# Longer rows for half of Q and K in a cross-covariance attention kernel

## The chip, the core and the metric

The kernel runs on one core of one Trainium2 chip. The metric is the device time of one execution in microseconds (us). Times are medians over several runs; beside them stands one profiled execution, from which all durations of single instructions come.

## The reference

For each of 8 x 12 = 96 heads, Q, K and V are 512 x 64 matrices in float32. The columns of Q and K are divided by their norms over the 512 rows, the 64 x 64 product of the two goes through a softmax over its last axis, and V is multiplied with the result:

```python
Q_norm = Q / (np.linalg.norm(Q, axis=-2, keepdims=True) + 1e-10)
K_norm = K / (np.linalg.norm(K, axis=-2, keepdims=True) + 1e-10)
attn = np.einsum('bhnd,bhne->bhde', Q_norm, K_norm)
attn = np.exp(attn - np.max(attn, axis=-1, keepdims=True))
attn = attn / (np.sum(attn, axis=-1, keepdims=True) + 1e-10)
return np.einsum('bhnd,bhde->bhne', V, attn)
```

Each of Q, K, V and the output is 12.58 MB, so that 37.75 MB are read and 12.58 MB are written.

## The kernel before, in words

**Units.** Four heads are a unit u (U = 24), two units a pair s (S = 12), two pairs a window w (W = 6, 16 heads each). A head's 512 rows lie on 32 partitions, 16 rows of 64 numbers on each (T = 16), so that a partition's share of Q or K of one unit is a contiguous stretch of 4 KB. V lies on 16 partitions a head, in stretches of 8 KB. The output is stored in stretches of 2 KB.

**Stages.** `load_qk` (L170) and `load_v` (L182) bring the inputs in, mostly 1 MB at a time, into the tiles `qk32` (3 buffers, a pair each) and `v32` (3 buffers). `cast_qk` (L196) writes q and k of a unit side by side, in bf16, into `qkb` (2 buffers), on VectorE. `grams` (L210) multiplies, for each head and each t, the 32 x 128 block [q|k] with itself: 64 matmuls a unit. The 128 x 128 sum holds the squared norms of the columns of q and k on its diagonal and q.k off it. It lies in the PSUM tile `gram`, four banks, one buffer, one pair at a time. `squares` (L222) and `sums` (L236) take the diagonals out on VectorE, `cross` copies the off-diagonal block on ScalarE, `powers` makes inverse norms as exp(-0.5 ln x) on ScalarE, `scale_k` (L248) scales the block on GpSimd, `logits` transposes it on TensorE, `exps` (L265) takes exponentials on ScalarE, and `normalise` (L272) divides by their sums on VectorE.

**V and the output.** `cast_v` makes bf16 of V, on GpSimd for the most part; `vtrans` transposes it on TensorE into a single-buffered PSUM tile, `vcopy` copies that to SBUF, `outs` (L298) multiplies with the attention, `ocopy` copies PSUM to the store tile `so` (13 buffers), and `store` writes 0.5 MB. The copies of one kind all go through `copy` (L162), whose lines L164, L166 and L168 are the ScalarE, the VectorE and the GpSimd form. For the last window, the quarters q >= TAIL of the transposed V are cut in halves, which use four further PSUM banks that become free when the last `gram` has been read (`late_pool`).

**Order.** All DMAs are issued by SyncE (SP in the profile), in one queue. The class `Order` lays out the program before it is emitted: every piece has a price on one or more engines, pieces that it comes after, and a rank (`R`); a simulated clock picks what starts next, and `BIAS` makes one engine less attractive than another. The resulting order on each engine is fixed, and each engine waits in that order. From pair `BOTH` (= 4) on, copies of the output and casts of V may go to either of two engines.

Of the kernel before, what the change touches and what calls it, by code (L numbers as in the profile page):

```python
# [8 lines left out]
F32 = mybir.dt.float32  # L9
BF16 = mybir.dt.bfloat16  # L10
# [3 lines left out]
D = 64  # L14
T = 16
# [87 lines left out]
def kernel(  # L103
# [12 lines left out]
    W = S // 2  # L116
    TAIL = 2
    WIDE = U - 1
    ONE = 3
    BOTH = S - 8  # L120

# [5 lines left out]

    Vu = V.rearrange("b h (p t) d -> (b h p) (t d)", t=2 * T).rearrange("(w r p) x -> w r p x", r=2, p=128)

# [7 lines left out]

    NB = dict(qk=3, v=3, vb=2, qkb=2, vt=2, so=13, sm=2, ab=4)
    const = ctx.enter_context(tc.tile_pool(name="const", bufs=1))
    qp = ctx.enter_context(tc.tile_pool(name="qp", bufs=NB["qk"]))  # L140
    vp = ctx.enter_context(tc.tile_pool(name="vp", bufs=NB["v"]))
    vbp = ctx.enter_context(tc.tile_pool(name="vbp", bufs=NB["vb"]))
    qkp = ctx.enter_context(tc.tile_pool(name="qkp", bufs=NB["qkb"]))
    vtp = ctx.enter_context(tc.tile_pool(name="vtp", bufs=NB["vt"]))
    sop = ctx.enter_context(tc.tile_pool(name="sop", bufs=NB["so"]))
# [3 lines left out]
    ps_o = ctx.enter_context(tc.tile_pool(name="ps_o", bufs=2, space=bass.MemoryType.PSUM))  # L149
    grams_only = ExitStack()  # L150
    ps_g = grams_only.enter_context(tc.tile_pool(name="ps_g", bufs=1, space=bass.MemoryType.PSUM))
    late = {}

    def late_pool():
# [3 lines left out]
        return late["p"]  # L158

    qk32, v32, vb, qkb, gram, scr, kq, n2, r8, kqs, rq, lg, ex, ab, vps, vt, po, so = ({} for _ in range(18))  # L160

# [7 lines left out]

    def load_qk(s, x, r):  # L170

        w, e = divmod(s, 2)
        if s not in qk32:
            qk32[s] = qp.tile([128, 2, 2, T, D], F32, name="qk32")
        if 2 * s + (r or 0) >= WIDE:
            nc.sync.dma_start(out=qk32[s][:, x, r].rearrange("p (m j) d -> p m (j d)", m=2), in_=(Qw, Kw)[x][U - 1])
        elif r is None:
            nc.sync.dma_start(out=qk32[s][:, x].rearrange("p r t d -> p r (t d)"), in_=(Qu, Ku)[x][w, e])
        else:
            nc.sync.dma_start(out=qk32[s][:, x, r].rearrange("p t d -> p (t d)"), in_=(Qu, Ku)[x][w, e, :, r])  # L180

# [14 lines left out]
    def cast_qk(u, x):  # L196
# [3 lines left out]
        nc.vector.tensor_copy(qkb[u][:, :, x * D:(x + 1) * D], qk32[s][:, x, r])  # L200

    def cast_v(eng, w, r, c):

        if w not in vb:
            vb[w] = vbp.tile([128, 2 * T, 2, D], BF16, name="vb")
        copy(eng, vb[w][:, c * T:(c + 1) * T, r], v32[w, r][:, c].rearrange("p (t d) -> p t d", d=D))

    def grams(u):


        s, r = divmod(u, 2)
        if r == 0:
            gram[s] = ps_g.tile([128, HU, 2, 2, 2 * D], F32, name="gram")
        for t in range(T if u < WIDE else J):
            for h in range(HU):
                if u < WIDE:
                    x = qkb[u][32 * h:32 * (h + 1), t, :]
                else:
                    x = qkb[u][64 * (h % 2):64 * (h % 2 + 1), J * (h // 2) + t, :]
                nc.tensor.matmul(gram[s][:, h, r, 0], x, x, start=(t == 0), stop=(t == (T if u < WIDE else J) - 1))  # L220

    def squares(s, n):  # L222

        if n == 0:
            scr[s] = small.tile([128, 2 * HU, D], F32, name="scr")
        half = (LO, HI)[n]
        nc.vector.scalar_tensor_tensor(  # L227
            out=scr[s][half], in0=gram[s][half, :, :, 0, half].rearrange("p h r d -> p (h r) d"), scalar=1e-20,
            in1=eye2[half, None, :].to_broadcast([D, 2 * HU, D]), op0=ALU.add, op1=ALU.mult,
        )  # L230

    def cross(eng, s):

        kq[s] = small.tile([128, 2 * HU, D], F32, name="kq")
        copy(eng, kq[s][HI], gram[s][HI, :, :, 0, LO].rearrange("p h r d -> p (h r) d"))

    def sums(s):
        n2[s] = small.tile([128, 2 * HU], F32, name="n2")
        nc.vector.tensor_reduce(out=n2[s], in_=scr[s], axis=mybir.AxisListType.X, op=ALU.add)  # L239

    def powers(s):

        ln = small.tile([128, 2 * HU], F32, name="ln")
        r8[s] = small.tile([128, 2 * HU], F32, name="r8")
        nc.scalar.activation(ln, n2[s], AF.Ln)
        nc.scalar.activation(r8[s], ln, AF.Exp, scale=-0.5)  # L246

    def scale_k(eng, s):  # L248
        kqs[s] = small.tile([128, 2 * HU, D], F32, name="kqs")
        (nc.vector if eng == "DVE" else nc.gpsimd).tensor_tensor(  # L250
            out=kqs[s][HI], in0=kq[s][HI], in1=r8[s][HI, :, None].to_broadcast([D, 2 * HU, D]), op=ALU.mult,
        )

    def scales_q(s):

        rq[s] = small.tile([128, HU], F32, name="rq")
        nc.scalar.copy(rq[s][LO], r8[s][LO, 0::2])
        nc.scalar.copy(rq[s][HI], r8[s][LO, 1::2])
# [64 lines left out]
    nc.gpsimd.tensor_tensor(out=eye2, in0=ident[:, :D], in1=ident[:, D:], op=ALU.add)  # L323

    abs_ = []
    for i in range(NB["ab"]):
# [4 lines left out]
    def size(key):  # L331
        if key[0] == "gr" and key[1] >= WIDE:
            return 64
        return 8 if key[0] == "vt" and key[-1] is not None else {"gr": 128, "lg": 8, "vt": 16, "ou": 16}[key[0]]

    plan = Order(size)
    X = 1.29
    R = dict(cq=2.5, gr=2.471, sq=0.756, kq=1, rd=3.457, pw=3.5, sc=1, rq=1.9, lg=5, ex=1.1, nm=2.545, cv=1.165, vt=0.9, vc=1.1, ou=2, oc=0.9)
    BIAS = dict(sc=-0.6, kq=5, cv=1, vc=-0.3, oc=0.6)
    QK_PACE, V_FROM, V_PACE, ST_LAG = 0.631, 0.0377, 0.7486, 1.5133  # L340

# [3 lines left out]
    def piece(key, engines, after, behind, rank, fn, *args):  # L345
        if key[0] in ("cv", "vc", "oc", "kq", "sc"):
            plan.add(key, engines, after, behind, rank, lambda eng: fn(eng, *args))
# [6 lines left out]

    def parts(s):
        return (0, 1) if s < ONE or s == S - 1 else (None,)

    def loaded(x, s, r):
        return ("l" + "qk"[x], s, r if len(parts(s)) == 2 else None)

    last = None
    for s in range(S):
        free = [back("cq", 2 * s + r, 2 * NB["qk"], x) for r in range(2) for x in range(2)]
        for r in parts(s):
            at = QK_PACE * (2 * s + (r or 0)) / U
            for x in range(2):
                key = loaded(x, s, r)
                piece(key, {"DMA": X if r is not None else 2 * X}, free, [last], at, load_qk, s, x, r)
                last = key
    for u in range(U):  # L370
        s, r = divmod(u, 2)
        piece(("cq", u, 0), {"DVE": 0.72}, [loaded(0, s, r), back("gr", u, NB["qkb"])], [back("cq", u, 1, 1)], R["cq"] + 0.01 * u, cast_qk, u, 0)
        piece(("cq", u, 1), {"DVE": 0.72}, [loaded(1, s, r)], [("cq", u, 0)], R["cq"] + 0.01 * u, cast_qk, u, 1)
        piece(("gr", u), {"PE": 1.6}, [("cq", u, 0), ("cq", u, 1), back("kq", s, 1)], [back("gr", u, 1)], R["gr"] + 0.01 * u, grams, u)
    for s in range(S):
        SM = NB["sm"]

        piece(("sq", s, 0), {"DVE": 0.70}, [("gr", 2 * s), ("gr", 2 * s + 1), back("rd", s, SM)], [], R["sq"] + 0.01 * s, squares, s, 0)
        piece(("sq", s, 1), {"DVE": 0.70}, [("gr", 2 * s), ("gr", 2 * s + 1)], [("sq", s, 0)], R["sq"] + 0.01 * s, squares, s, 1)
        piece(("kq", s), {"ACT": 0.60, "DVE": (0.70, BIAS["kq"])}, [("sq", s, 0), ("sq", s, 1), back("sc", s, SM)], [], R["kq"] + 0.01 * s, cross, s)  # L380
        piece(("rd", s), {"DVE": 0.69}, [("sq", s, 0), ("sq", s, 1), back("pw", s, SM)], [], R["rd"] + 0.01 * s, sums, s)
        piece(("pw", s), {"ACT": 0.5}, [("rd", s), back("rq", s, SM), back("sc", s, SM)], [], R["pw"] + 0.01 * s, powers, s)
        piece(("sc", s), {"POOL": (1.04, BIAS["sc"]), "DVE": 1.2}, [("pw", s), ("kq", s), back("lg", s, SM)], [], R["sc"] + 0.01 * s, scale_k, s)
        piece(("rq", s), {"ACT": 0.45}, [("pw", s), back("ex", s, SM)], [], R["rq"] + 0.01 * s, scales_q, s)
        piece(("lg", s), {"PE": 0.6}, [("sc", s), back("ex", s, 1)], [], R["lg"] + 0.01 * s, logits, s)
        piece(("ex", s), {"ACT": 1.30}, [("lg", s), ("rq", s), back("nm", s, NB["sm"])], [], R["ex"] + 0.01 * s, exps, s)
        piece(("nm", s), {"DVE": 1.12}, [("ex", s)] + [back("ou", s, NB["ab"], x) for x in range(4)], [], R["nm"] + 0.01 * s, normalise, s)
# [83 lines left out]
```

## Time and profile before

| | us |
|---|---|
| median of 3 runs (130.26 to 130.95) | 130.85 |
| the profiled execution's own time | 130.86 |
| its span, first to last instruction | 129.1 |
| VectorE (DVE) busy | 91.0 (71%) |
| TensorE (PE) busy | 77.8 (60%) |
| ScalarE (ACT) busy | 72.5 (56%) |
| GpSimd (POOL) busy | 37.3 (29%) |
| time of the DMA packets, as a share of 16 engines' span | 98.0% |

A busy time is the sum of an engine's instructions; for DMA it is the mean over the core's 16 DMA engines. The own time of the profiled execution stands 1.8 us above its span and is equal to the median.

### The profile page before, as it was taken

How to read it: one execution, taken by the hardware profiler on the slowest of the kernel's cores; microseconds unless marked ns; L12 is line 12 of the kernel's file. 1: busy time of each engine (PE TensorE's matmuls, PEld its weight loads, DVE VectorE, ACT ScalarE, POOL GpSimd, SP SyncE). 2: the span in 40 equal slices, each digit the busy share in tenths (PEclk: the TensorE clock that was granted, in tenths of full speed). 3: DMA queues.
4: the chain of work that ended last, by engine and by line, in shares of the span. 5: the costliest groups of instructions: out<-in, count | busy, mean ns of one | idle time of the engine just before them, and what ended most of it. 6: DMA issues, size and time to landing. Idle time of an engine off the chain costs nothing.

```text
span 129.1 us, 4881 instructions
## 1 busy us (share of the span) xinstructions
PE 77.8 (60%) x2128; PEld 63.3 (49%) x2128; DVE 91.0 (71%) x140; ACT 72.5 (56%) x220; POOL 37.3 (29%) x39
## 2 busy tenths in 40 slices
PE   0154384994837648967682986697785858382000
PEld 0144372773636537856572865486664746271000
DVE  3444649849999389699986798997999799830000
ACT  3000441569777085497783798383947969973000
POOL 3005406300813914043058003223463270300000
PEclk9999999999975685599999599655799999955555
DMA  4999999999999999999999999999999999999982
GB/s 133 389 430 410 432 399 409 408 416 409 422 406 411 404 408 410 402 413 430 410 414 406 416 415 418 405 420 415 405 410 403 405 399 406 402 407 406 408 312 75
DMA packets 15605, 50.64 MB, mean 392 GB/s; under 512 B 1120, under 2 KB 1632, under 8 KB 14176
## 3 DMA queue, kind: packets, MB, share of 16 engines
q1 hardware_dynamic: 15584, 50.34, 98.0%
q8 instruction: 16, 0.26, 0.8%
q14 instruction: 5, 0.04, 0.1%
HBM read 37.75 MB, written 12.58 MB: 390 GB/s over the span
## 4 chain that ended last, share of the span: by engine, by line
DMA 50%; DVE 16%; PE 10%; ACT 8%; issue 3%; SPq 1%; POOL 1%; ACTq 0%; POOLq 0%; DVEq 0%
DMA qk<-in_K_dram 21%; DMA v<-in_V_dram 15%; DMA qk<-in_Q_dram 14%; DVE qkb L200 7%; PE gram L220 6%; ACT so L164 3%; DVE scr L227 3%; DVE vt L166 2%; PE po L306 2%; DVE ab L278 2%; PE vps L289 2%; ACT ex L269 2%; ACT vt L164 2%; DVE n L239 1%; SPq L180 1%
## 5 line engine op out<-in xcount | busy, mean ns | idle before, releaser
L220 PE MATMUL gram<-qkb 32*128 32x128 bf16 (+1 forms) x1504 | 36.6, 259 | 21.7 <-DVE qkb L200 15.4
L200 DVE CAST qkb<-qk 128x1024 bf16<-128x1024 f32 x48 | 37.4, 799 | 11.7 <-DMA qk<-in_Q_dram 5.2
L220 PEld LDWEIGHTS <-qkb 32*128 32x128 bf16 (+1 forms) x1504 | 30.5, 116 | 26.8 <-DVE qkb L200 18.1
L168 POOL TENSOR_SCALAR vb<-v 128x1024 bf16<-128x1024 f32 x19 | 21.9, 1162 | 46.7 <-DMA v<-in_V_dram 46.4
L164 ACT COPY so<-po 128x512 f32<-128x512 f32 x45 | 25.0, 592 | 7.6 <-PE po L306 7.5
L164 ACT COPY vt<-vps 128x1024 bf16<-128x1024 bf16 (+1 forms) x18 | 17.8, 987 | 16.9 <-PE vps L289 16.8
L306 PE MATMUL po<-ab,vt 128*64 128x128 bf16 x384 | 21.3, 260 | 6.7 <-issue 2.8
L250 POOL TENSOR_TENSOR kqs<-kq,r 64x512 f32<-64x512 f32 x12 | 14.2, 1179 | 26.1 <-ACT r L246 14.1
L306 PEld LDWEIGHTS <-vt 128*64 128x64 bf16 x384 | 15.5, 131 | 10.8 <-issue 5.8
L289 PE MATMUL vps<-identb,vb 128*128 128x128 bf16 x192 | 16.7, 236 | 6.6 <-POOL vb L168 3.9
L227 DVE SCALAR_TENSOR_TENSOR scr<-gram,eye 64x512 f32<-64x512 f32 x24 | 16.5, 688 | 5.6 <-PE gram L220 5.3
L289 PEld LDWEIGHTS <-vb 128*128 128x128 bf16 x192 | 12.6, 105 | 9.6 <-POOL vb L168 4.9
L269 ACT ACTIVATE ex<-lg,rq 128x64 f32<-128x64 f32 x48 | 14.5, 322 | 2.8 <-PE lg L263 2.8
L164 ACT COPY kq<-gram 64x512 f32<-64x512 f32 x12 | 7.0, 581 | 14.4 <-DVE scr L227 14.0
L278 DVE TENSOR_TENSOR ab<-ex,rinv 64x256 bf16<-64x256 f32 x24 | 13.5, 560 | 0.6
L269 ACT ACTIVATION_READ_ACCUMULATOR ex<-lg,rq 128x1 f32 x48 | 10.2, 213 | 0.0
L263 PE MATMUL lg<-eye,kqs 64*128 64x64 f32 x48 | 6.6, 266 | 4.1 <-POOL kqs L250 2.8
L239 DVE TENSOR_REDUCE n<-scr 128x8 f32<-128x512 f32 x12 | 8.1, 678 | 0.1
L166 DVE COPY vt<-vps 128x1024 bf16<-128x1024 bf16 (+1 forms) x8 | 7.9, 1019 | 0.1
L263 PEld LDWEIGHTS lg<-eye,kqs 64*128 64x128 f32 x48 | 4.7, 162 | 6.0 <-POOL kqs L250 3.6
L166 DVE CAST vb<-v 128x1024 bf16<-128x1024 f32 x5 | 5.1, 1012 | 0.9 <-DMA v<-in_V_dram 0.9
L275 DVE RECIPROCAL rinv<-esum 128x4 f32<-128x4 f32 x12 | 2.1, 171 | 2.5 <-ACT ex L269 2.5
(15 smaller groups left out, 15.8 us busy)
## 6 DMA issues: line engine op xcount, KB each, us to landing
out_dram<-so SPq DMA_DIRECT2D x23, 512.0 KB, 10.2
v<-in_V_dram SPq DMA_DIRECT2D x11, 1024.0 KB, 17.9
qk<-in_Q_dram SPq DMA_DIRECT2D x8, 1024.0 KB, 18.2
qk<-in_K_dram SPq DMA_DIRECT2D x8, 1024.0 KB, 18.8
qk<-in_Q_dram SPq DMA_DIRECT2D x8, 512.0 KB, 12.1
qk<-in_K_dram SPq DMA_DIRECT2D x8, 512.0 KB, 12.5
v<-in_V_dram SPq DMA_DIRECT2D x2, 512.0 KB, 10.7
out_dram<-so SPq DMA_DIRECT2D x2, 256.0 KB, 9.1
```

The costliest lines, as they stand in the source:

```text
L164: nc.scalar.copy(o, i)
L166: nc.vector.tensor_copy(o, i)
L168: nc.gpsimd.tensor_scalar(out=o, in0=i, scalar1=1.0, scalar2=0.0, op0=ALU.mult, op1=ALU.add)
L200: nc.vector.tensor_copy(qkb[u][:, :, x * D:(x + 1) * D], qk32[s][:, x, r])
L220: nc.tensor.matmul(gram[s][:, h, r, 0], x, x, start=(t == 0), stop=(t == (T if u < WIDE else J) - 1))
L227: nc.vector.scalar_tensor_tensor(out=scr[s][half], in0=gram[s][half, :, :, 0, half].rearrange("p h r d -> p (h r) d"), scalar=1e-20, in1=e ...
L250: (nc.vector if eng == "DVE" else nc.gpsimd).tensor_tensor(out=kqs[s][HI], in0=kq[s][HI], in1=r8[s][HI, :, None].to_broadcast([D, 2 * HU, ...
L263: nc.tensor.transpose(l[:, h, :], kqs[s][HI, 2 * h:2 * h + 2].rearrange("p r d -> p (r d)"), eye2[HI])
L269: nc.scalar.activation(e[:, h, :], lg[s][:, h, :], AF.Exp, scale=rq[s][:, h:h + 1], accum_out=z[:, h:h + 1])
L278: nc.vector.tensor_tensor(out=a[half, :, half], in0=e[half], in1=ri[half, :, None].to_broadcast([D, HU, D]), op=ALU.mult,)
L289: nc.tensor.transpose(ps[:, c, n, :], vb[w][:, J * c + j].rearrange("p r d -> p (r d)"), identb)
L306: nc.tensor.matmul(po[s, x][e * D:(e + 1) * D, j].rearrange("p r d -> p (r d)"), v, ab[s][:, h, :])
```

## The change

Windows 2, 3 and 4 (48 heads) are now "big". Their Q and K are loaded with a head on 16 partitions, 32 rows on each, so that a partition's stretch is 8 KB; a pair `m` is then eight heads, and its two units are the two halves of each partition's rows. The 32 partitions of a matmul now hold two heads. `mask_q` writes two copies of the bf16 q, in each of which the rows of one of the two heads are zero, and `big_grams` multiplies [q|k] with the 128 columns of the two copies. That gives the norms of q and the products k.q of both heads, but no norms of k. Those come from `square_k` (squares of the float32 k, ScalarE), `fold_k` (sums over a partition's 32 rows, GpSimd or VectorE) and `norms_k` (a matmul that adds a head's 16 partitions). The later steps of a big window run once for 16 heads, where they ran once for 8.

The tile `qkb` has 4 buffers instead of 2, `so` 9 instead of 13. TAIL is 4 instead of 2, so that nothing of the last window is cut in halves and no further PSUM banks are used. BOTH is 0 instead of 4. The ranks, biases and paces of the plan have other values. The `gram` tile keeps its four banks; for a big window it holds all four units.

```diff
-    TAIL = 2
+    TAIL = 4
-    BOTH = S - 8
+    BIG = (2, 3, 4)
+    BOTH = S - 12
...
+    Vu, Qb, Kb = (
+        x.rearrange("b h (p t) d -> (b h p) (t d)", t=2 * T).rearrange("(w r p) x -> w r p x", r=2, p=128)
+        for x in (V, Q, K))
...
-    NB = dict(qk=3, v=3, vb=2, qkb=2, vt=2, so=13, sm=2, ab=4)
+    NB = dict(qk=3, v=3, vb=2, qkb=4, vt=2, so=9, sm=2, ab=4)
+    mqp = ctx.enter_context(tc.tile_pool(name="mqp", bufs=NB["qkb"]))
+    ksp = ctx.enter_context(tc.tile_pool(name="ksp", bufs=1))
...
+        if big(m):
+            nc.sync.dma_start(out=qk32[m][:, x].rearrange("p c t d -> p (c t d)"), in_=(Qb, Kb)[x][w, e])
...
+    def mask_q(u):
+        mqb[u] = mqp.tile([128, T, 2, D], BF16, name="mqb")
+        for a in range(2):
+            nc.vector.tensor_scalar(
+                out=mqb[u][:, :, a], in0=qkb[u][:, :, :D], scalar1=half_of[:, a:a + 1], scalar2=None, op0=ALU.mult)
+    def square_k(u):
...
+        nc.scalar.activation(ksq[m][:, c], qk32[m][:, 1, c], AF.Square)
+    def fold_k(eng, m, part):
+        e = nc.vector if eng == "DVE" else nc.gpsimd
+        if part == 0:
+            e.tensor_tensor(out=ksq[m][:, 0], in0=ksq[m][:, 0], in1=ksq[m][:, 1], op=ALU.add)
+            return
+        ksum[m] = small.tile([128, D], F32, name="ksum")
+        n = T // 2
+        while n:
+            o = ksq[m][:, 0, :n] if n > 1 else ksum[m][:, None, :]
+            e.tensor_tensor(out=o, in0=ksq[m][:, 0, :n], in1=ksq[m][:, 0, n:2 * n], op=ALU.add)
+            n //= 2
+    def norms_k(m):
...
+        nc.tensor.matmul(o[:, :, r], ksum[m], head_of, start=True, stop=True)
+    def big_grams(u):
...
+        for t in range(T):
+            for n in range(HU):
+                rows = slice(32 * n, 32 * (n + 1))
+                o = g[:, n, :4 * D].rearrange("p (a r d) -> p a r d", a=2, r=2)[:, :, r]
+                nc.tensor.matmul(o, qkb[u][rows, t], mqb[u][rows, t], start=(c == 0 and t == 0), stop=(c == 1 and t == T - 1))
+    def big_squares(w):       # VectorE, 64 x 1024
+    def big_cross(eng, w):    # ScalarE or VectorE, 64 x 1024
+    def big_sums(w):          # VectorE, 64 x 1024
+    def logs_k(w):            # ScalarE, Ln of the norms of k, 64 x 16
+    def big_powers(w):        # ScalarE, Ln of those of q, Exp of both
+    def big_scale_k(eng, w):  # GpSimd or VectorE, 64 x 1024
+    def big_scales_q(w):      # ScalarE, two copies
...
+    half_of, head_of: two reductions of ident on VectorE; eye4, tiny: a copy and a memset on GpSimd
...
-    BIAS = dict(sc=-0.6, kq=5, cv=1, vc=-0.3, oc=0.6)
-    QK_PACE, V_FROM, V_PACE, ST_LAG = 0.631, 0.0377, 0.7486, 1.5133
+    BIAS = dict(ka=5, sc=0, kq=5, cv=5, vc=0.3, oc=0.6)
+    QK_PACE, V_FROM, V_PACE, ST_LAG = 0.5767, 0.076, 0.5601, 1.0571
...
+        if m >= NB["qk"] and big(m - NB["qk"]):
+            free += [("ks", 2 * (m - NB["qk"]) + i) for i in range(2)]
...
+            wait, release = release, [("kQ", w), ("sQ", w), ("lK", w)] if big(m) else [("kq", m)]
...
+        if big(m):
+            piece(("mq", u), {"DVE": 0.66}, [("cq", u, 0), back("gr", u, NB["qkb"])], [], R["mq"] + 0.01 * u, mask_q, u)
+            free = [("ka", before, 1)] if i == 0 and before is not None else []
+            piece(("ks", u), {"ACT": 1.15}, [loaded(1, m, i)] + free, [back("ks", u, 1)] if i else [], R["ks"] + 0.01 * u, square_k, u)
+            if i == 1:
+                for n in range(2):
+                    piece(("ka", m, n), {"POOL": 2.15, "DVE": (1.15, BIAS["ka"])}, ..., R["ka"] + 0.02 * m, fold_k, m, n)
+                piece(("kn", m), {"PE": 0.3}, [("ka", m, 1)], [("gr", 4 * w + 3)], R["kn"] + 0.02 * m, norms_k, m)
+        piece(("gr", u), {"PE": 1.6}, [("cq", u, 0), ("cq", u, 1), ("mq", u) if big(m) else None] + wait, [back("gr", u, 1)],
+              R["gr"] + 0.01 * u, big_grams if big(m) else grams, u)
```

The new functions from `big_squares` on are given by their names, engines and sizes; each is one or two instructions of the kind that its counterpart before has.

## The prediction

> **What bounds the kernel now.** I read the page's DMA lines first, because the engines' shares (71% at most) name no bound.
>
> ```profile
> DMA  4999999999999999999999999999999999999982
> ...
> DMA packets 15605, 50.64 MB, mean 392 GB/s; under 512 B 1120, under 2 KB 1632, under 8 KB 14176
> ...
> q1 hardware_dynamic: 15584, 50.34, 98.0%
> ```
>
> From the second slice to the last but one, all 16 DMA engines are busy, and their packets take 98.0% of 129.1 us. 15605 less 14176 leaves 1429 packets of 8 KB and more: the 11 V loads of 1 MB have 11 x 128 = 1408 stretches of 8 KB, and the 21 packets of the instruction queues make up the rest. So a packet is a partition's stretch, and the rate by size can be read from stretches in which one kind of load is served. These lines are from the table of stretches (columns: stretch, its length, busy PE, PEld, DVE, ACT, POOL, PE clock, DMA share, GB/s):
>
> ```profile
> 18.00:26.00 8.00, 5.93 (x148) 4.69 (x150) 6.35 (x10) 3.20 (x13) 3.14 (x3) 1.00 1.02 408
> 42.00:50.00 8.00, 4.75 (x136) 3.98 (x136) 5.59 (x11) 4.29 (x14) 3.68 (x4) 0.71 1.02 401
> 62.00:66.00 4.00, 2.83 (x102) 2.34 (x100) 3.90 (x6) 3.34 (x6) 0.18 (x1) 1.00 1.00 415
> 34.00:95.00 61.00, 44.21 (x1216) 35.73 (x1204) 52.72 (x78) 41.36 (x129) 22.11 (x19) 0.78 1.02 412
> 95.00:118.00 23.00, 15.26 (x356) 12.32 (x355) 17.25 (x30) 18.67 (x57) 6.20 (x6) 0.88 1.05 405
> ```
>
> The DMA queue serves in order, and a 1 MB load lands 18 us after its issue (page, part 6). By the issue times, 18 to 26 and 42 to 50 carry Q and K in 4 KB stretches (408 and 401 GB/s), and 62 to 66 two V loads in 8 KB stretches (415). The last two lines are for the engines: in the middle VectorE is busy for 52.7 of 61 us, so DMA is the bound, but not by much. The chain of waits agrees: 50% of it is DMA, and from 32.5 to 91 us it runs over three loads end to end.
>
> How late may the engines be? The last copy of output ends at 117.4 us, the last store is issued at 119.3, and it needs 9.1 us (median of the two quarter stores) because the queue is full. The shortest load, with an empty queue, landed in 3.3 us. So the work at the end has about 9.1 - 3.3 = 5.8 us to spare.
>
> [...] the trace shows more, 401 to 408 against 415, 1.7 to 3.5%. [...] a cast behind the scaling on GpSimd (1.33 us from 49.92) starts at 50.36 and lasts 1.44 us, where its median is 0.69. [...] the trace's copy of 1024 from PSUM takes 1.01.
>
> ```profile
> L200 DVE CAST qkb<-qk 128x1024 bf16<-128x1024 f32 x48 | 37.4, 799 | 11.7 <-DMA qk<-in_Q_dram 5.2
> ...
> L250 POOL TENSOR_TENSOR kqs<-kq,r 64x512 f32<-64x512 f32 x12 | 14.2, 1179 | 26.1 <-ACT r L246 14.1
> ...
> L227 DVE SCALAR_TENSOR_TENSOR scr<-gram,eye 64x512 f32<-64x512 f32 x24 | 16.5, 688 | 5.6 <-PE gram L220 5.3
> ...
> L278 DVE TENSOR_TENSOR ab<-ex,rinv 64x256 bf16<-64x256 f32 x24 | 13.5, 560 | 0.6
> ```
>
> **The change, part by part.**
>
> *DMA.* 48 heads of Q and K are 12.58 MB, in 1536 packets instead of 3072. At 404.5 GB/s (between 401 and 408) they take 31.1 us, at 415 30.3: 0.8 us less. The ends: [...] 1.06 us by 401. Number, size and order of kinds of the DMAs on SP's queue stay, so this is on the path from end to end.
>
> *VectorE.* Added: 24 tensor_scalar of 1024 bf16. No row shows one. [...] Gone: 12 `squares` x 0.688 = 8.3 [...] 6 `sums` x 0.678 = 4.1 for 3 x 1.21 = 3.6. Sum +3.3 us.
>
> *ScalarE.* Added: 12 squares of 1024 x 1.04 = 12.5 us. Gone on balance: 0.5 of `cross` (6 x 0.581 for 3 x 1.01), 1.3 of `powers` less 0.7 for `logs_k`, 1.2 of `scales_q`. Sum +10.2.
>
> *GpSimd.* From `scale_k`, 1.04 us for 512 at best, an add costs 2.03 ns an element: 2.1 us for the first (1024), 2.2 for the ladder (960, and three more starts), 4.3 a pair, 25.8 for six. Three wide scalings for six take 0.9 away. [...]
>
> *The lock.* Now casts lose 48 x (799 - 694) = 5.0 us and `normalise` 24 x (560 - 422) = 3.3, 0.115 us for each of 72, with GpSimd busy 22.1/61 = 36%. With the folds it is (22.1 + 24.9)/61 = 77%, so at least 2.1 times the wait, 0.245, for 24 casts, 24 masks and 12 halves of `normalise`: 14.7, where 36 x 0.115 = 4.1 stood, thus +10.6. The upper end: the folds last twice as long, so the residual wait may double: +25. I take +11[...].
>
> *Sum in the middle stage (34 to 95).* VectorE and ScalarE are busy for 52.7 + 41.4 = 94.1 of 122 us. Added 3.3 + 10.2 + 11 = 24.5: 118.6. BOTH = 0 lets copies of 15 us (8.0 vt, 5.1 vb, 2.1 so on VectorE) move between them. The densest 10 us slice now (30 to 40) holds 9.42 + 8.16 = 17.6 of 20, 88%. At 88% the stage takes 118.6/(2 x 0.88) = 67.4 us, 6.4 late. Loads run ahead by more than a 1 MB load's 18 us, and stores fill in, so DMA is not starved there. The next stage has 17.3 + 18.7 = 36 of 46 us; at 88% it takes 20.5 for 23 and gives 2.5 back. Late at the end: 3.9 us.
>
> *Waits and buffers.* TAIL = 4: the last two quarters go through one bank, 0.62 + 1.01 + hops = 1.75 us each, about 1 us more than the halves. 3.9 + 1 = 4.9, inside 5.8. The first gram after a big window waits for squares, cross and the logs of k; behind it on TensorE stand transposes, logits and outs; K's landing to logs is 2 squares, 4.3 of folds, 0.3 and 0.25, about 7 us, which four cast buffers and an idle TensorE (60%) cover. `qk32` is freed only after ScalarE's squares too, 2.1 us, covered by the loads ahead. `ksq` has one buffer: a square waits for the last pair's fold, and output copies and exponentials wait behind it on ScalarE; folds take 4.3 of the roughly 10 us of a pair, so at zero unless GpSimd is late. `so` with 9: a store is issued each 1.29 us and lands after 10.2, so 8 are in flight; one is left for the copy, which then runs at DMA's pace. The six small matmuls (0.3 each) and constants cost nothing: VectorE idles 2.15 us before its first cast[...]; GpSimd idles until 11.15.
>
> So the gain of 0.8 stays: 130.86 - 0.8 = 130.1, and as the profiled execution equals the median, 130.1 for the runs too.
>
> **The rivals.**
>
> *The lock decides (slower).* One mechanism: folds on GpSimd hold VectorE's casts and masks. If the lock costs 18 us instead of 11 (midway to the upper end), the stage is 7/(2 x 0.88) = 4.0 us later: 8.9 - 5.8 = 3.1 beyond the slack, 133.2. It turns at 12.6 us of lock, 1.6 above my value. For it: VectorE at 86% already and waits that end with GpSimd's instruction. Against it: some 21 us of VectorE's idle time now end with an event of DMA, PE or ACT (its waits, summed), and part of the lock's wait falls into such gaps.
>
> *The gain is eaten (same).* [...] the end is late by up to a microsecond: 130.3 to 131.4, at 130.8.
>
> *Rows do nothing (same): the change doesn't do what it says.* If 415 against 404 comes from what runs beside it, no gain: 130.9. 60 to 80 us, which mixes sizes, shows 415 to 417 too, which speaks for this a little.
>
> *Nine store buffers with one square buffer (slower).* ScalarE blocked in turn by stores and folds: some 2 us, 132.
>
> **How the numbers follow.** Half a percent, 0.65 us, is about what a measurement of this kernel can tell from no change. Forecast 0.44 (of which 0.04 falls within 0.5%); eaten or nothing 0.18; lock 0.32; buffers 0.06. Faster 0.40, same 0.22, slower 0.38. The forecast's own range is 129.7 to 130.4; over all, 129.5 (gain 1.06 and a little from the tail) to 133.2, the lock's value.
>
> **What would show it.** Right: 1536 packets fewer under 8 KB, 415 GB/s where big loads are served, DMA at 9 in all slices, mask mean below 0.5 us, last output copy before 122 us and the last store still 5 us or more from issue to landing. Wrong: VectorE above 105 us with casts above 1.0 us on average and GpSimd over 60 us; DMA slices under 9 between 80 and 125 us; the chain of waits on GpSimd's folds instead of loads; or a last store that lands 3 us after its issue, which says that the engines set the end.

## The result, and the profile after

The changed kernel takes 146.64 us (median of 4 runs) against 130.90 for the kernel before (4 runs beside it): ratio 1.121, interval 1.114 to 1.128. The forecast was 130.1, the top of the range 133.2. Some runs of the kernels below took over 1.5% longer than the fastest of the same kernel; ratios leave them out, and where they would change a reading, they are given apart.

From the page of the changed kernel: the DMA slices and rates, the packets, the DMA queue, and four of the costliest groups.

```profile
DMA  5999999999999999999999999998699845247796
GB/s 181 370 411 428 402 413 410 419 414 423 412 414 412 419 409 430 409 420 426 396 432 421 364 406 402 335 338 304 152 347 406 307 150 218 80 149 290 282 373 214
DMA packets 14069, 50.64 MB, mean 350 GB/s; under 512 B 1120, under 2 KB 1632, under 8 KB 11104
...
q1 hardware_dynamic: 14048, 50.34, 88.9%
...
L212 DVE CAST qkb<-qk 128x1024 bf16<-128x1024 f32 x48 | 43.3, 937 | 6.2 <-DMA qk<-in_Q_dram 4.8
...
L237 POOL TENSOR_TENSOR ksq<-ksq 128x512 f32<-128x512 f32 (+2 forms) x18 | 20.8, 1154 | 1.4
L231 POOL TENSOR_TENSOR ksq<-ksq 128x1024 f32<-128x1024 f32 x6 | 15.0, 2503 | 11.8 <-ACT lnk L280 6.4
...
L218 DVE TENSOR_SCALAR mqb<-qkb,half_of 128x1024 bf16<-128x1024 bf16 x24 | 17.4, 765 | 0.2
```

The rows did what the diff says: 15605 - 14069 = 1536 packets fewer. But from the 26th slice (some 90 us) the rate falls, and from the 28th (98 us) the DMA engines' share too. VectorE is busy for 119.6 us instead of 91.0, GpSimd for 78.8 instead of 37.3. The same by stretch (columns as before: length, busy PE, PEld, DVE, ACT, POOL, PE clock, DMA share, GB/s):

```profile
34.00:95.00 61.00, 35.70 (x989) 29.76 (x982) 56.52 (x67) 35.12 (x74) 42.69 (x33) 0.76 1.01 407
95.00:118.00 23.00, 14.09 (x335) 11.79 (x335) 21.81 (x26) 12.62 (x31) 19.81 (x16) 0.63 0.83 292
118.00:140.00 22.00, 15.16 (x368) 11.88 (x356) 18.31 (x30) 19.98 (x66) 7.14 (x5) 1.00 0.59 219
```

In the middle, DMA is still full because loads had been issued ahead, but the engines do less: TensorE 989 matmuls where 1216 were done, ScalarE 74 instructions where 129 were (big windows need fewer of them: 92 in e1 below). ScalarE is not short of time (35.1 of 61 us); VectorE nearly is (56.5), and GpSimd has doubled. The debt comes due mostly when only stores are left: the last store is issued at 140.0 us, where it was at 119.3.

The chain of waits, followed back from the end, has changed owner; these are its shares of the span before and after:

```profile
DMA 50%; DVE 16%; PE 10%; ACT 8%; issue 3%; SPq 1%; POOL 1%; ACTq 0%; POOLq 0%; DVEq 0%
```

```profile
DVE 51%; DMA 27%; PE 12%; issue 3%; ACT 1%; SPq 1%; DVEq 0%
```

Here is a piece of the timeline of the changed kernel, VectorE and GpSimd alone (columns: start, length, engine, line, operation; other engines' lines are left out):

```profile
98.61 2.26 DVE L212 CAST qkb<-qk 128x1024 bf16<-128x1024 f32 x2
98.84 5.28 POOL L175 TENSOR_SCALAR vb<-v 128x1024 bf16<-128x1024 f32 x4
...
101.38 1.84 DVE L218 TENSOR_SCALAR mqb<-qkb,half_of 128x1024 bf16<-128x1024 bf16 x2
...
103.14 1.52 DVE L212 CAST qkb<-qk 128x1024 bf16<-128x1024 f32 x1
104.09 2.77 POOL L231 TENSOR_TENSOR ksq<-ksq 128x1024 f32<-128x1024 f32 x1
104.70 3.24 DVE L286 TENSOR_TENSOR kqs<-scr,r 64x1024 f32<-64x1024 f32 x1
```

A cast of 0.69 us (median in the kernel before and in this one) lasts 1.52 while GpSimd casts V; the wide scaling, which the plan has moved to VectorE here, starts in a fold of 2.77 us and lasts 3.24, where it takes 1.58 without folds (e1 below). This lengthening is what the prediction and the expectations call the lock. That GpSimd holds something that VectorE needs was the author's assumption; the runs show how long the instructions take.

### The profile page after: what moved, and what is told of

It reads as the page before. It is cut to its first block, busy times and chain, and to the rows that moved or that the text cites. A ratio compares the mean times of both kernels' runs of the same rounds, so it can differ in the third digit from the quotient of the medians.

```text
span 144.8 us, 4941 instructions
## 1 busy us (share of the span) xinstructions
PE 81.2 (56%) x2140; PEld 67.2 (46%) x2140; DVE 119.6 (83%) x160; ACT 78.9 (55%) x210; POOL 78.8 (54%) x70
## 2 busy tenths in 40 slices
DMA packets 14069, 50.64 MB, mean 350 GB/s; under 512 B 1120, under 2 KB 1632, under 8 KB 11104
## 4 chain that ended last, share of the span: by engine, by line
DVE 51%; DMA 27%; PE 12%; issue 3%; ACT 1%; SPq 1%; DVEq 0%
DMA qk<-in_Q_dram 22%; DVE qkb L212 18%; DVE mqb L218 10%; DMA qk<-in_K_dram 5%; DVE kqs L286 4%; DVE ab L376 4%; DVE so L173 4%; PE gram L260 4%; DVE vt L173 3%; DVE scr L264 2%; PE vps L387 2%; PE po L404 2%; PE gram L317 2%; DVE n L273 2%; ACT so L171 1%
## 5 line engine op out<-in xcount | busy, mean ns | idle before, releaser
L175 POOL TENSOR_SCALAR vb<-v 128x1024 bf16<-128x1024 f32 x24 | 31.3, 1325 | 11.6 <-DMA v<-in_V_dram 11.4
L317 PE MATMUL gram<-qkb 32*128 32x128 bf16 (+1 forms) x736 | 18.5, 272 | 16.2 <-DVE qkb L212 16.2
L171 ACT COPY so<-po 128x512 f32<-128x512 f32 x35 | 19.5, 590 | 10.6 <-PE po L404 10.3
L317 PEld LDWEIGHTS <-qkb 32*128 32x128 bf16 (+1 forms) x736 | 16.0, 123 | 17.9 <-DVE qkb L212 17.3
L171 ACT COPY vt<-vps 128x1024 bf16<-128x1024 bf16 x18 | 18.2, 1014 | 9.0 <-PE vps L387 9.0
L237 POOL TENSOR_TENSOR ksq<-ksq 128x512 f32<-128x512 f32 (+2 forms) x18 | 20.8, 1154 | 1.4
L231 POOL TENSOR_TENSOR ksq<-ksq 128x1024 f32<-128x1024 f32 x6 | 15.0, 2503 | 11.8 <-ACT lnk L280 6.4
L367 ACT ACTIVATE ex<-lg,rq 128x64 f32<-128x64 f32 x48 | 14.5, 317 | 12.5 <-PE lg L361 12.3
L260 PE MATMUL gram<-mqb,qkb 32*128 32x128 bf16 x768 | 17.6, 259 | 4.8 <-DVE qkb L212 3.3
L348 POOL TENSOR_TENSOR kqs<-scr,r 64x512 f32<-64x512 f32 x5 | 5.4, 1084 | 25.0 <-ACT r L344 16.6
L260 PEld LDWEIGHTS <-qkb 32*128 32x128 bf16 x768 | 15.3, 116 | 6.3 <-DVE qkb L212 3.8
L218 DVE TENSOR_SCALAR mqb<-qkb,half_of 128x1024 bf16<-128x1024 bf16 x24 | 17.4, 765 | 0.2
L225 ACT ACTIVATE ksq<-qk 128x1024 f32<-128x1024 f32 x12 | 12.5, 1058 | 7.8 <-POOL ksum L237 7.8
## 6 DMA issues: line engine op xcount, KB each, us to landing
v<-in_V_dram SPq DMA_DIRECT2D x11, 1024.0 KB, 15.8
```

What stands on the lines that cost most here:

```text
L171: nc.scalar.copy(o, i)
L175: nc.gpsimd.tensor_scalar(out=o, in0=i, scalar1=1.0, scalar2=0.0, op0=ALU.mult, op1=ALU.add)
L218: nc.vector.tensor_scalar(out=mqb[u][:, :, a], in0=qkb[u][:, :, :D], scalar1=half_of[:, a:a + 1], scalar2=None, op0=ALU.mult)
L231: e.tensor_tensor(out=ksq[m][:, 0], in0=ksq[m][:, 0], in1=ksq[m][:, 1], op=ALU.add)
L237: e.tensor_tensor(out=o, in0=ksq[m][:, 0, :n], in1=ksq[m][:, 0, n:2 * n], op=ALU.add)
L260: nc.tensor.matmul(o, qkb[u][rows, t], mqb[u][rows, t], start=(c == 0 and t == 0), stop=(c == 1 and t == T - 1))
```

## The experiments

"Last store" is the issue of the last DMA of output in the profiled run; "VectorE" is its busy time there. The spread of the kernel before over these runs is 130.35 to 131.15 in its medians.

### The two halves of the change alone

**e4_rows_only.** The kernel before with

```diff
+        elif s // 2 in (2, 3, 4):
+            nc.sync.dma_start(out=qk32[s][:, x].rearrange("p r t d -> p (r t d)"), in_=(Qb, Kb)[x][w, e])
```

> The kernel before, loading Q and K of windows 2 to 4 in 8 KB stretches and computing on as if they lay as before, which mixes heads. It is the gain of the rows alone: 0.8 us less by the prediction (ratio 0.994), [...] none if the rate is set by something else.

Measured: ratio 0.9953 (0.9934 to 0.9972), 130.02 against 130.69 us: 0.61 us less, between 0.37 and 0.86. Its DMA slices are full throughout, as they were. The gain is real and was sized well.

**e3_before_buffers.** The kernel before with

```diff
-    TAIL = 2
+    TAIL = 4
-    BOTH = S - 8
+    BOTH = S - 12
-    NB = dict(..., so=13, ...)
+    NB = dict(..., so=9, ...)
-    grams_only = ExitStack()
+    grams_only = ctx.enter_context(ExitStack())
```

> The kernel before with 9 store buffers instead of 13, TAIL 4 and BOTH 0, and none of the longer rows. If buffers and tail are innocent, 130.5 to 132 us. If the nine buffers or the single bank carry the loss, 136 us or more.

Measured: ratio 1.0051 (1.0022 to 1.0079), 131.31 us. These three settings move the last store from 119.3 to 123.9 us and cost 0.7 us, not 15. Which of the three does it was not tried.

### The folds on GpSimd

**e1_short_folds.** All adds of `fold_k` but one of 64 elements are left out:

```diff
         if part == 0:
-            e.tensor_tensor(out=ksq[m][:, 0], in0=ksq[m][:, 0], in1=ksq[m][:, 1], op=ALU.add)
             return
...
-        n = T // 2
-        while n:
-            ...
+        e.tensor_tensor(out=ksum[m][:, None, :], in0=ksq[m][:, 0, :1], in1=ksq[m][:, 1, :1], op=ALU.add)
```

> The changed kernel with the sums of k's squares cut from five adds to one of 64 elements on GpSimd; the norms of k are left wrong by that, all else and the order on every engine stay. If the folds decide (by the lock or by their length), the 36 us of GpSimd work go, VectorE falls from 119.6 us busy to below 105, and the time to 129.5 to 133 us. If the nine store buffers, the single bank at the end or the new order decide, it stays at 143 to 147 us.

Measured: 130.83 us, ratio 0.9995 (0.9972 to 1.0018); VectorE 99.7 us, last store 123.1. The folds carry all of the loss. The middle stretch, with the columns of the table above:

```profile
34.00:95.00 61.00, 42.57 (x1203) 35.06 (x1199) 57.26 (x87) 43.74 (x92) 23.56 (x23) 0.81 1.02 414
```

VectorE is as busy there as with the folds, 57.3 us for 56.5, but it gets 87 instructions done instead of 67. The granted clock of TensorE isn't the cause: it was 0.764 to 0.787 in the runs of the changed kernel, but the profiled run of e1 had 0.768 and took 130.69 us.

Of VectorE's instructions none was taken away, and yet it is busy for 19.9 us less in the whole run. The two lines each are of VectorE's groups, the first pair from this kernel and the second from e2, where the folds run:

```profile
L212 DVE CAST qkb<-qk 128x1024 bf16<-128x1024 f32 x48 | 33.2, 726 | 8.5 <-DMA qk<-in_Q_dram 4.9 <-DMA qk<-in_K_dram 3.2
L218 DVE TENSOR_SCALAR mqb<-qkb,half_of 128x1024 bf16<-128x1024 bf16 x24 | 13.8, 616 | 0.2
```

```profile
L212 DVE CAST qkb<-qk 128x1024 bf16<-128x1024 f32 x48 | 43.3, 934 | 7.0 <-DMA qk<-in_Q_dram 3.9 <-DMA qk<-in_K_dram 2.7
L218 DVE TENSOR_SCALAR mqb<-qkb,half_of 128x1024 bf16<-128x1024 bf16 x24 | 19.4, 848 | 0.2
```

**e2_detached_folds.** The adds work on a constant tile, and the squares are written in bf16 and read by nobody, so that nobody waits for the folds:

```diff
+        ksum[m] = some_sum
-            e.tensor_tensor(out=ksq[m][:, 0], in0=ksq[m][:, 0], in1=ksq[m][:, 1], op=ALU.add)
+            e.tensor_tensor(out=spare, in0=spare, in1=spare, op=ALU.add)
...
-            e.tensor_tensor(out=o, in0=ksq[m][:, 0, :n], in1=ksq[m][:, 0, n:2 * n], op=ALU.add)
+            e.tensor_tensor(out=spare[:, :n], in0=spare[:, :n], in1=spare[:, n:2 * n], op=ALU.add)
```

> The changed kernel with the five adds on GpSimd kept in size and place, but working on a constant tile, so that nothing waits for them (the norms of k come from a constant; the squares are written in bf16 and read by nobody). Theory of the lock: GpSimd still holds VectorE's casts and masks, VectorE stays above 112 us busy, and the time stays at 140 us or more. Rival, that the chain squares, folds, norms, logs is too long: with nobody waiting for the folds the time falls to 129.5 to 134 us.

Measured: 143.68 us, ratio 1.100 (1.095 to 1.105); VectorE 118.3 us, last store 137.4. Without any wait for a fold, 12.9 of the 15.8 us between e1 and the changed kernel are there. Could it be GpSimd's own queue, the V casts and scalings behind the folds? These are all waits of TensorE for GpSimd in e2 (columns: engine, line, released by: us in total, times, longest):

```profile
PEld lg L360 <- POOL kqs L347: 2.8, 2, 2.4
...
PE lg L360 <- POOL kqs L347: 2.4, 2, 2.2
...
PEld L386 <- POOL vb L175: 1.3, 2, 0.9
...
PE vps L386 <- POOL vb L175: 0.9, 2, 0.6
```

In e1 the same four are 2.4, 2.0, 1.5 and 1.1, so TensorE doesn't wait longer for GpSimd. ScalarE waits for it in neither; the DMA queue waits 3.1 us for it in e2 and not at all in e1. What is left is that the same VectorE instructions take 18.6 us longer while GpSimd works: casts 10.1, masks 5.6, scalings 1.7, `normalise` 1.2. The other kinds are not longer: output copies, which read PSUM, take 687 ns in e1 and 686 in e2, `sums` 678 and 676, `squares` 688 in both. So it is these four kinds that get longer and not VectorE as a whole; by what means GpSimd does it, no run shows.

In the changed kernel the DMA queue waits 17.3 us for casts of V on GpSimd, and the last two V loads are issued from 101.8 us on, where it is 96.6 in e2: late folds hold up the casts behind them too.

**e6_no_masks.** The folds stay, and the masks go:

```diff
-            nc.vector.tensor_scalar(out=mqb[u][:, :, a], ...)
...
-                nc.tensor.matmul(o, qkb[u][rows, t], mqb[u][rows, t], ...)
+                nc.tensor.matmul(o, qkb[u][rows, t], qkb[u][rows, t, None, :D].to_broadcast([32, 2, D]), ...)
```

> The changed kernel without the 24 masks (the unmasked q is multiplied twice, which mixes two heads); folds stay on GpSimd. If it is VectorE that is late, the 17.4 us that the masks take on it go and the time falls by 10 us or more, to 130 to 136 us. If it is GpSimd that is late (its own queue of folds, V casts and scalings), the time stays at 142 us or more.

Measured: 139.18 us (the other run, 142.59); VectorE 99.3 us, last store 132.4. Both expectations fail: VectorE is no busier than in e1, and the kernel is still 8 us slower than the one before. The casts still take 0.91 us, and the waits show a second way:

```profile
ACT ksq L221 <- POOL ksum L233: 9.8, 4, 4.8
PEld gram L245 <- POOL ksum L233: 7.6, 3, 3.0
PE gram L245 <- POOL ksum L233: 7.2, 3, 2.9
```

Squares wait on ScalarE for the one `ksq` buffer, which the last fold still reads, and the norms of k wait on TensorE. So there is a second cause: the chain from squares over folds to the norms of k, whose folds GpSimd finishes late.

**e11_detached_no_masks.** e2 and e6 together.

> Folds detached as in e2 and masks left out as in e6, both together; it mixes heads and takes the norms of k from a constant. GpSimd keeps its 36 us of folds and the lock. If VectorE's lateness and the wait for the folds are two causes of which each alone holds the time above 140 us, taking both away gives 129.5 to 133 us. If GpSimd's own queue (V casts and scalings behind the folds) is a third, 137 us or more.

Measured: 135.98 us, ratio 1.039 (1.029 to 1.050); VectorE 106.5 us, last store 129.9. The four form a square: 146.6 (all), 143.7 (no chain), 139.2 (no masks), 136.0 (neither). The chain is worth 3.0 us with masks and 3.2 without, the masks 7.4 with the chain and 7.7 without; these differences are rough, for there is one run of e6 and the two of e11 lie 1.6 apart. The time lies between the two expected ranges, and some 5 us above e1 remain. They are again on VectorE: casts average 1.05 us, and TensorE's waits for GpSimd are those of e1 (1.9, 1.5, 1.5, 1.0 us), so the third cause that was offered isn't seen.

**e5_split_folds.** The same adds in pieces of at most 256 elements:

```diff
+            for q in range(4):
+                t = slice(4 * q, 4 * q + 4)
+                e.tensor_tensor(out=ksq[m][:, 0, t], in0=ksq[m][:, 0, t], in1=ksq[m][:, 1, t], op=ALU.add)
```

> The changed kernel with the folds on GpSimd cut into adds of at most 256 elements (about 0.5 us each instead of up to 2.1), same sums. If VectorE loses time because it waits for whole GpSimd instructions, shorter ones cost it less: casts fall from 0.94 us to below 0.85, VectorE from 119.6 to below 113 us, the time to 136 to 143 us. If the total of GpSimd's work is what counts, it stays at 144 us or more.

Measured: 148.11 us (the other run, 151.51); VectorE 113.3 us, last store 141.4. VectorE is busy for 6 us less, but casts stay at 0.91. GpSimd rises to 85.3 us, and squares wait 12.5 us for folds instead of 7.8. No remedy.

**e10_real_prices.** `{"POOL": (2.5, 4.3)[n], "DVE": (1.15, 9.0)}` instead of `{"POOL": 2.15, "DVE": (1.15, BIAS["ka"])}`.

> The changed kernel planned with GpSimd prices of 2.5 and 4.3 us for the two parts of a fold (2.15 and 2.15 in the change; the trace shows 2.5 and 3.9 plus gaps), and nothing else. If the loss comes from an order laid out for folds that take longer than planned, a plan with real prices wins back much of it: below 140 us. If the work and the lock themselves do not fit, 143 us or more.

Measured: 152.1 us, ratio 1.163 (1.153 to 1.173). A plan that knows how long folds last is worse. The bias against VectorE rose too, from 5 to 9, and the ranks had been made for other prices; which of these does it was not tried.

### The folds elsewhere

**e8_vector_folds.** `{"DVE": 1.15}` as the only engine.

> The changed kernel with the folds on VectorE alone. No lock from folds, [...] VectorE at 112 to 117 us busy. From 99.7 us with 130.8 and 119.6 us with 146.6, one us of VectorE is worth one us beyond about 104: 138 to 144 us. If only the lock mattered and not VectorE's own time, 131 to 134 us.

Measured: 155.85 us, ratio 1.191 (1.179 to 1.202); VectorE 122.0 us, beyond both. The order was laid out anew, so this mixes work and order.

**e7_tensor_folds.** Squares in bf16 with two buffers, no folds, and

```diff
-        nc.tensor.matmul(o[:, :, r], ksum[m], head_of, start=True, stop=True)
+        for c in range(2):
+            for t in range(T):
+                nc.tensor.matmul(o[:, :, r], ksq[m][:, c, t], head_ofb, start=(c == 0 and t == 0), stop=(c == 1 and t == T - 1))
...
-                for n in range(2):
-                    piece(("ka", m, n), ...)
-                piece(("kn", m), {"PE": 0.3}, [("ka", m, 1)], [("gr", 4 * w + 3)], ...)
+                piece(("kn", m), {"PE": 2.5}, [("ks", u - 1), ("ks", u)], [("gr", u)], ...)
```

> The changed kernel with the folds moved to TensorE: squares are written in bf16 and 32 matmuls a pair add over rows and partitions at once, so GpSimd has no folds. The result is complete. Lock theory: VectorE at 99 to 102 us busy and 130 to 132 us in all, like the kernel with the sums left out. Rival, that TensorE's queue becomes the bound with 192 more matmuls[...]: 134 us or more.

Measured: 140.82 us, ratio 1.079 (1.071 to 1.087); VectorE 102.0, GpSimd 40.3 us; the 192 matmuls keep TensorE busy for 8.2 us. Without folds on GpSimd the kernel is still slow; matmuls and order both changed here.

**e9_tensor_folds_same_order.** The same matmuls, with the `ka` pieces left in the plan but emitting nothing.

> The folds on TensorE as in e7, but planned at the changed kernel's prices for them, so that every engine keeps the changed kernel's order; the result is complete. If e7 was slow because the plan was laid out anew with ranks made for other prices, this one runs like the kernel with the sums left out, 130 to 132.5 us, with about 8 us more on TensorE. If the 192 matmuls themselves cost (TensorE late), 136 us or more.

Measured: 132.57 us (the other three, 135.78 to 137.08; no interval); in the profiled run, of 137.08 us, VectorE 105.0 us, last store 128.7. The kept order is worth 5 us or more against e7; e1's 130.83 isn't shown to be out of reach, but none of the four runs has it.

**e12_one_matmul.** e9 with one matmul a pair.

> e9 with one matmul a pair for the norms of k instead of 32, which leaves most of the sum out; squares, order and everything else stay. If the five us between e9 and the kernel with short folds are the 192 matmuls on TensorE (9.6 us busy), it falls to 130.5 to 132 us. If VectorE sets the time (105 us busy in e9, 99.7 with short folds), it depends on VectorE alone: unchanged near 135 us if that stays at 105.

Measured: 130.01 us, ratio 0.9919 (0.9891 to 0.9947); VectorE 103.3 us, last store 121.3. With loads, masks, squares and order all in place but without the sum of k's squares, the kernel is faster than before. What separates it from e9 is 186 matmuls of 8 columns (all 192: 9.6 us busy on TensorE in e9), while VectorE is nearly as busy. So "VectorE alone sets the time" falls too. The 186 cost 2.6 us by e9's run of 132.57.

**e14_half_early** and **e15_half_early_vector_add.** For the first pair of a big window, the matmuls go ahead of the third unit's gram; e15 also adds the two halves of the squares on VectorE and keeps 16 matmuls a pair:

```diff
     def big_grams(u):
+        if r == 1 and c == 0:
+            add_k(m - 1, 0)
+            add_k(m - 1, 1)   # not in e15
```

> e9 with the 32 matmuls of each big window's first pair moved ahead of the third unit's gram, when TensorE is less pressed; the same 192 in all, result complete. If the place decides (64 in a row, 3.5 us, before the next window may start), it falls by half of the 5 us or more, to 131 to 133 us. If the total on TensorE decides, it stays at 135 to 136 us.

> e14 with the two halves of the bf16 squares first added on VectorE (6 adds of 1024[...]), so that 16 matmuls a pair are left; result complete. If TensorE's row of matmuls is what is late, 130 to 131.5 us. If VectorE has no room for 3.7 us more (103 to 105 us busy already), 132 us or more.

Measured: e14 132.91 us (the other three, 135.41 to 137.19; no interval), e15 133.66 us, ratio 1.023 (1.018 to 1.028), last store 126.6. Half of the row moved away changes nothing (132.91 for 132.57), so its place isn't what counts. That the number counts isn't shown: e15, with half as many matmuls, is no faster, and its own 4.9 us on VectorE (6 adds, 0.82 us each) are in it. In e9 and in e14 the shortest run is the one with the highest mean granted clock of TensorE (0.876 and 0.858; the six others 0.769 to 0.842), while in 20 runs of e12, from 0.754 to 0.884, time doesn't go with the clock; that points to TensorE, on few runs. Whether it is the matmuls' own time or something else that goes with 373 more instructions (5259 in e9, 4886 in e12) stays open. No complete version was found that beats the kernel before.

## Why the prediction was wrong

**Right: the bound, the rows, the slack.** DMA bounded the kernel, and 48 heads in 8 KB stretches save 0.61 us where 0.8 stood (upper end 1.06). The stretches that gave 0.8 were not pure, by the landings: the one from 18 us holds 1.7 us of a V load, the one from 62 holds 1.2 of a K load. But the landings agree. In the traces of both kernels all 70 DMAs land in the order of their issue; in the kernel before, a load of 1 MB of Q or K lands 2.55 us after the DMA ahead of it (median), one of V 2.48, and with the long rows Q and K take 2.48 too (e4; 2.49 in the changed kernel). The slack at the end was 5.8 us: the last store now comes 140.0 - 119.3 = 20.7 us later, and 20.7 - 5.8 = 14.9, near the measured 15.7. Over the other kernels: last store at 121.3 (e12) and 123.1 (e1), spans 128.1 and 128.9; at 128.7 (e9) and 137.4 (e2), spans 135.2 and 142.2. The span stands still up to about 123 us and then follows the last store.

**Right in kind, wrong in size: the lock.** The rival said that folds on GpSimd lengthen VectorE's casts and masks, and e1 against e2 shows it: casts from 0.73 to 0.93 us, masks from 0.62 to 0.85 (means). Three terms were short. The folds occupy GpSimd for 15.0 + 10.1 + 5.5 + 5.1 + 2.9 = 38.6 us, not 25.8; whether VectorE's work makes them longer in turn, no run sets apart. VectorE loses 18.6 us to them (e2 less e1), where 11 was taken between 10.6 and 25. And a mask takes 0.48 us at the median in e1 (0.47 at least), 24 x 0.48 = 11.5 us, more than I had put into the +3.3 for VectorE; mine was an estimate that no row of the kernel before showed. Near what I took were ScalarE's 12 squares, 1.06 us each in the changed kernel (12.5 in all), and VectorE's wide `squares`, 1.21, and `sums`, 1.20. Of the signs of being wrong, VectorE above 105 us, GpSimd above 60 and the gaps of the DMA came; so did a last store that lands soon, 3.9 us after its issue (9.1 before); casts, at 0.94 us, stayed under the 1.0 named, and the chain runs over VectorE, not over the folds.

**Wrong: the sum over two engines.** This is the step that failed. It put VectorE and ScalarE into one account, 118.6 of 122 us, and so divided lateness by two, on the ground that copies of 15 us could move off VectorE. By this account the 18.6 us that were measured are worth 18.6/(2 x 0.88) = 10.6 us; from e1 to e2 the last store moves by 14.3. And the rival's 18 us gave 133.2 us, where 146.6 came. Nor did the next stage give 2.5 us back: VectorE is busy for 21.8 of its 23 us. Of the last store's 20.7 us, 3.8 are there without folds (e1), 14.3 come with the lock (e2) and 2.6 with the chain; the prediction had 4.9 in all. (Its densest slice, for the 88%, wasn't 30 to 40 us but 100 to 110, with 18.0 of 20; 90% would have made it milder still.)

The fixed order moves the other way: these are VectorE's copies of output before and after, 3 and 13,

```profile
L166 DVE COPY so<-po 128x512 f32<-128x512 f32 x3 | 2.1, 687 | 0.5 <-PE po L306 0.5
```

```profile
L173 DVE COPY so<-po 128x512 f32<-128x512 f32 x13 | 8.7, 685 | 2.5 <-PE po L404 2.4
...
L286 DVE TENSOR_TENSOR kqs<-scr,r 64x1024 f32<-64x1024 f32 x2 | 6.5, 3250 | 0.1
```

and two of three wide scalings and a narrow one, 8.1 us that I had left on GpSimd (BIAS sc went from -0.6 to 0). Only V casts, 5.1 us, left. This costs nothing alone, since e1 has the same order and loses nothing, but it takes the room away. VectorE's rise is 28.6 us: masks 17.4, scalings 8.1, output copies 6.6, casts of q and k 5.9, `normalise` 1.2, less 5.1 for V casts, 5.0 for squares and sums, and 0.5 of small terms and rounding. I had 14.3. Counted on VectorE alone, even that would have been too much: 52.7 + 14.3 = 67.0 us of work in a stage of 61 is 6.0 late with no gap at all, and the slack was 5.8. ScalarE, busy for 35.1 us of the stage where 41.4 was, did not help: in this stage it waits 17.5 us for TensorE and 7.4 for folds, and TensorE waits 16.6 us for VectorE.

**Wrong: the chain at nothing.** I costed the single `ksq` buffer at zero "unless GpSimd is late". It is late: squares wait 7.8 us for folds, and the V casts and V loads behind the folds are late as well. Taking the chain away is worth some 3 us, with masks (e2) or without (e11 against e6).

**Right: the small matter.** Buffers, tail and BOTH cost 0.7 us (e3); I had named one microsecond for the tail and hidden it in the slack. The rival "nine store buffers with one square buffer" has no share from the former beyond that.

**Not settled.** The loss, 15.8 us from e1, divides into some 3 for the chain, 7.7 that go with the masks and 5 that stay when both are gone, but this rests on one or two runs each. Nor is it settled why 186 small matmuls cost 2.6 us or more on an engine that is busy for 71.2 of the 101 us after 34 us (e9).

## What to carry to other kernels

When DMA is the bound, compute that is added is free only up to the slack of the engine that receives it (here 5.8 us at the end); find that slack from the last store (when it is issued, how long it waits) and count lateness on each engine alone, in the order that is fixed, not on a sum of engines. An instruction moved to GpSimd wasn't off VectorE's account here: 35.8 us more work on GpSimd made VectorE's casts, masks, scalings and `normalise` 18.6 us longer (e1 against e2), so price the pair, and look at where a planner's biases will put the work. Try a part that can be had alone (here the rows, 0.5%) before building the machinery around it.

## What was not expected of the hardware

The ladder's adds of 512, 256, 128 and 64 elements took 1.69, 0.92, 0.85 and 0.48 us on GpSimd in the changed kernel, and in e6 the one of 256 took 1.44; the one of 128 took from 0.45 to 2.32 us in the changed kernel. So short instructions are lengthened too, and cutting the folds up (e5) made GpSimd busier, 85.3 us for 78.8. And a matmul with 8 columns and 64 weights was listed with 0.19 us (9.6 us for 192 in e9), little below the 0.25 of one with 128 columns there.
